# Column sums of every tile at the five block transitions, and the last norm in one pass

## The chip, the cores and the metric

The kernel runs on one core of a Trainium2 chip. The metric is the time of one execution on the device in microseconds (us). The engines are called by their short names: PE is TensorE (matmuls), with PEld for its weight loads, DVE is VectorE, ACT is ScalarE, POOL is GpSimd, and SP issues the DMAs.

## What is computed

Two transformer blocks follow each other on 256 tokens with a model width of 1024, in float32. The first block has two layers, each a mixer (sparse attention in layer 0, differential attention in layer 1) and a squared-ReLU MLP; after each of the four the residual goes through a layer norm. The second block puts 16 meta tokens ahead, and has a mixer and an MLP with RMS norms. The parts that the change touches:

```python
def layer_norm(x, g, b):
    mu = jnp.mean(xf, axis=-1, keepdims=True)
    var = jnp.mean(jnp.square(xf - mu), axis=-1, keepdims=True)
    return ((xf - mu) * lax.rsqrt(var + EPS) * g + b)

# first block, each layer l
        y = ...mixer(modulate(x, sh1, sc1))
        x = layer_norm(ALPHA * x + (1.0 + g1[:, None, :]) * y, ln_g[l, 0], ln_b[l, 0])
        y = sq_relu_mlp(modulate(x, sh2, sc2), mlp_w1[l], mlp_w2[l])
        x = layer_norm(ALPHA * x + (1.0 + g2[:, None, :]) * y, ln_g[l, 1], ln_b[l, 1])

# second block
    h = jnp.concatenate([meta, x], axis=1)
        u = rms_norm_2(h, norm_mix_pre[l])
        proj = u @ w_in[l]
        ...
        h = h + rms_norm_2(mix, norm_mix_post[l])
        u = rms_norm_2(h, norm_mlp_pre[l])
```

Where an RMS norm follows a layer norm (the last layer norm of the first block and the first norm of the second), or where one RMS norm's result is added and goes into the next, the kernel needs the mean square of the second norm's input as well.

## The kernel before

Activations stand feature-major: the residual `xa` is eight tiles of 128 features x 256 tokens. A float32 product is taken as three matmuls on a high and a low half of each operand (`mm3`, lines 387 to 389: high-high, high-low, low-high); the halves of the weights, called `hi` and `lo`, are made on chip from the loaded `raw` by ACT (`cast_hi`) and by DVE or POOL (`cast_lo`, L352).

A *transition* is the end of a projection, the norm behind it, and the start of the next stage. There are five, and all go through `tail`: T0 (attention's output of layer 0), T1 (MLP of layer 0), T2 (differential attention's output of layer 1), T3 (MLP of layer 1, followed by `last_ln`) and T4 (the second block's output projection, followed by `post_norm`). In `tail` PE's order is written by hand: the eight output tiles y are finished in the order m = 0, 2, 4, 6, 1, 3, 5, 7, where n counts them. For n below 4 a tile gets the three matmuls of the last weight; from n = 4 on also those of the weights before it, six or nine in all. Ahead of the last three matmuls of each tile `finish[1](n, m, None)` is called, and after them `finish[1](n, m, y[m])`. DVE, ACT and POOL take their order from a scheduler that walks the program by priorities and dependences.

For the layer norms (`ln_finish`) each finished tile becomes r = y * gate + xa on DVE (`zn`, L633) and its square on ACT (`sq`, L635). The mean and mean square over the 1024 features need sums over partitions and over tiles. `totals` adds the tiles up: r on DVE and sq on POOL (lines 556 and 559, tile `run`). The column sums over partitions are matmuls on PE with the summed tile as weights and a column of ones as the moving operand (`col_sum`, two fp32 matmuls of 128 tokens each, written to a PSUM tile `tr`). They are taken three times for each quantity: for the sum of tiles n = 0 to 3, for that of 4 to 6, and for tile 7. The first stands ahead of the last three matmuls of tile n = 7, the other two behind them, with fillers (`warm`, a matmul of zeros with 512 columns) between. `rstd_rows` makes mean and 1/sigma from the sums and spreads them to rows of all partitions, on PE.

`last_ln` has two passes. It normalizes r in place (L1763, L1766), squares the result times g plus b on ACT (L1768), and takes column sums of all eight squares; from these come the scale of the second norm (`rstd_rows` again), and then the second block's input, `full` (L1779, L1781), with its halves `hh` and `hl`. At the same time POOL makes the new residual `xa` (L1777). The next stage multiplies `hi` and `lo` by `hh` and `hl` (tile `y`), and one feature tile of the weights by the meta tokens repeated eight times, `oh` and `ol` (tile `a`).

The meta tokens' halves `oh` and `ol` are made by POOL in two operations of 128 x 1024, L1704 and L1705, which the program has ahead of the second MLP. `post_norm` sums three quantities: y * post * xa (`full`) on POOL, and y^2 and (y * post)^2 (`sq`, `sqn`) on DVE.

## Time and profile before

| | |
|---|---|
| median of three runs | 1166.39 us (1165.0 to 1170.65) |
| the profiled execution | 1162.97 us |
| its span, first to last instruction | 1161.2 us |
| mean granted clock of PE in it | 0.955 of full speed |
| busy: PE, DVE, ACT, POOL | 92%, 72%, 51%, 23% |
| chain of waits: PE, DVE, DMA, POOL | 68%, 14%, 5%, 5% |

The profile is one execution, whose times are counted from the start of its span. In a timeline a row is one or several equal instructions of an engine, with the start, the time from the first start to the last end, and in brackets how long the engine stood idle before and what it waited for. Matmuls overlap their neighbours, so the price of one is read from the distance of the starts. PEclk in a table of windows is the clock that PE was granted, 1.00 for 2.4 GHz and 0.50 for 1.2 GHz.

### The profile page before, as it was taken

Reading aid. Unit: us, or ns where it says so; the run is one execution under the profiler, and the core shown is the slowest. Engines: PE = TensorE matmul, PEld = TensorE weight load, DVE = VectorE, ACT = ScalarE, POOL = GpSimd, SP = SyncE. Lnnn points to the kernel's source line nnn. Section 1 sums busy time; section 2 is a strip of 40 time slices with the busy share of each in tenths; the row PEclk is TensorE's granted clock in tenths of the full one; section 3 lists DMA queues with packets and bytes.
Section 4 is the critical chain, followed back from the end, with each engine's and each line's share of the span. In section 5 each row is a group of like instructions: output and inputs, shape, how many; then the busy total and the mean of one; then the engine's idle time right before and its main releaser. Section 6 shows DMA issues by size and latency. Waiting matters only on the chain.

```text
span 1161.2 us, 20465 instructions
## 1 busy us (share of the span) xinstructions
PE 1073.1 (92%) x7766; PEld 975.4 (84%) x7766; DVE 840.5 (72%) x1672; ACT 595.3 (51%) x1240; POOL 269.3 (23%) x307
## 2 busy tenths in 40 slices
PE   2789889999999999997999999998899989999996
PEld 1667667999999978896999999887776888899995
DVE  7578985799886677877976555678986677655553
ACT  2456747464445445653754444557365354544442
POOL 3284673100000201324000000336644250000000
PEclk9799888999999989997999999899899997999998
DMA  9977643299996227636587553032120252765621
GB/s 344 316 266 271 210 155 112 89 404 349 331 336 229 97 90 294 211 135 235 202 287 237 183 179 119 1 109 92 55 66 27 92 200 68 252 189 182 189 83 37
DMA packets 60447, 212.58 MB, mean 183 GB/s; under 512 B 6619, under 2 KB 9084, under 8 KB 60348
## 3 DMA queue, kind: packets, MB, share of 16 engines
q1 hardware_dynamic: 59424, 209.43, 51.3%
q0 software_dynamic: 192, 0.79, 0.4%
q8 instruction: 61, 1.00, 0.3%
q10 hardware_dynamic: 732, 1.05, 0.3%
q14 instruction: 38, 0.31, 0.1%
HBM read 209.15 MB, written 1.84 MB: 182 GB/s over the span
## 4 chain that ended last, share of the span: by engine, by line
PE 68%; DVE 14%; DMA 5%; POOL 5%; issue 4%; ACT 3%; POOLq 0%; DVEq 0%; ACTq 0%; SPq 0%
PE y L387 10%; PE y L388 10%; PE y L389 10%; PE pj L387 7%; PE pj L389 7%; PE pj L388 7%; DMA raw<-in_ws 3%; PE tr L392 2%; DVE lo L352 2%; PE y L401 2%; DVE raw L478 1%; PE y L392 1%; PE pj L392 1%; DVE cva L2178 1%; POOL se L1457 1%
## 5 line engine op out<-in xcount | busy, mean ns | idle before, releaser
L366 DVE TENSOR_TENSOR lo<-raw,hi 128x1024 fp32r<-128x1024 f32 (+1 forms) x208 | 226.6, 1105 | 107.0 <-ACT hi L365 106.9
L365 ACT ACTIVATE hi<-raw 128x1024 fp32r<-128x1024 f32 (+1 forms) x208 | 195.3, 959 | 94.1 <-PE pj L388 76.4
L387 PE MATMUL pj<-hh,hi 128*128 128x256 f32 x768 | 216.7, 282 | 0.3
L388 PE MATMUL pj<-hl,hi 128*128 128x256 f32 x768 | 216.6, 282 | 0.2 <-DVE hl L611 0.2
L389 PE MATMUL pj<-hh,lo 128*128 128x256 f32 x768 | 215.7, 281 | 0.0
L352 DVE TENSOR_TENSOR lo<-raw,hi 128x1024 fp32r<-128x1024 f32 (+2 forms) x103 | 126.6, 1236 | 42.2 <-ACT hi L347 40.8
L387 PEld LDWEIGHTS pj<-hh,hi 128*128 128x128 f32 x768 | 145.1, 189 | 2.5 <-ACT relu L807 0.9
L388 PEld LDWEIGHTS pj<-hl,hi 128*128 128x128 f32 x768 | 144.9, 189 | 1.6 <-DVE hl L611 0.4
L389 PEld LDWEIGHTS pj<-hh,lo 128*128 128x128 f32 x768 | 145.2, 189 | 0.0
L388 PE MATMUL y<-actl,hi 128*128 128x256 f32 x512 | 144.3, 282 | 0.8 <-DVE actl L810 0.7
L387 PE MATMUL y<-acth,hi 128*128 128x256 f32 x512 | 144.0, 281 | 0.0
L389 PE MATMUL y<-acth,lo 128*128 128x256 f32 x512 | 143.7, 281 | 0.0
L352 POOL TENSOR_TENSOR lo<-raw,hi 128x512 fp32r<-128x512 f32 (+3 forms) x28 | 47.5, 1703 | 357.9 <-ACT hi L347 335.9
L347 ACT ACTIVATE hi<-raw 128x1024 fp32r<-128x1024 f32 (+2 forms) x107 | 110.8, 1043 | 27.1 <-DMA raw<-in_ws 16.1
L478 DVE CUSTOM_DVE_ANT_0 raw<-raw,cact 128x1024 f32<-128x1024 f32 x75 | 97.1, 1303 | 2.7 <-DMA raw<-in_ws 2.7
L388 PEld LDWEIGHTS y<-actl,hi 128*128 128x128 f32 x512 | 96.9, 189 | 1.5 <-DVE actl L810 1.4
L387 PEld LDWEIGHTS y<-acth,hi 128*128 128x128 f32 x512 | 97.1, 190 | 0.1
L389 PEld LDWEIGHTS y<-acth,lo 128*128 128x128 f32 x512 | 96.8, 189 | 0.0
L388 PE MATMUL y<-hl,hi 128*128 128x256 f32 x296 | 84.5, 286 | 0.0
L387 PE MATMUL y<-hh,hi 128*128 128x256 f32 x264 | 79.7, 302 | 3.9 <-ACT f L1588 2.2
L809 ACT ACTIVATE acth<-act 128x256 fp32r<-128x256 f32 x96 | 39.4, 416 | 83.5 <-DVE act L808 83.5
L389 PE MATMUL y<-hh,lo 128*128 128x256 f32 x264 | 76.8, 291 | 0.0
(658 smaller groups left out, 2486.3 us busy)
## 6 DMA issues: line engine op xcount, KB each, us to landing
raw<-in_ws SPq DMA_DIRECT2D x372, 512.0 KB, 4.7
bm<-bscr SPq DMA_DIRECT2D x4, 512.0 KB, 14.6
raw<-in_ws SPq DMA_DIRECT2D x4, 416.0 KB, 8.7
bm<-in_ws SPq DMA_DIRECT2D x3, 512.0 KB, 8.2
raw<-in_ws SPq DMA_DIRECT2D x3, 408.0 KB, 3.7
zn<-in_ws SPq DMA_DIRECT2D x2, 512.0 KB, 6.6
xa<-in_xT SPq DMA_DIRECT2D x2, 512.0 KB, 6.6
oh<-in_ws SPq DMA_DIRECT2D x2, 512.0 KB, 7.3
```

What stands on the lines that cost most here:

```text
L347: return self.nc.scalar.activation(w[1], w[0], AF.Copy)
L352: return eng.tensor_tensor(w[2][:, a:b], w[0][:, a:b], w[1][:, a:b].bitcast(F32), op=OP.subtract)
L365: i = nc.scalar.activation(hi[:, a:b], raw[:, a:b], AF.Copy)
L366: j = (lo_by or nc.vector).tensor_tensor(lo[:, a:b], raw[:, a:b], hi[:, a:b].bitcast(F32), op=OP.subtract)
L387: mm(out, lh, rh, start=start, stop=False, skip_group_check=True)
L388: mm(out, lh, rl, start=False, stop=False, skip_group_check=True)
L389: mm(out, ll, rh, start=False, stop=stop, skip_group_check=True)
L392: self.nc.tensor.matmul(out, l, r, start=start, stop=stop, skip_group_check=True)
L401: last = self.nc.tensor.matmul(out, l, r, start=start, stop=stop, skip_group_check=True)
L478: nc.vector.tensor_tensor_reduce(out=raw, in0=raw, in1=self.cact, op0=OP.mult, op1=OP.add, scale=0.5, scalar=0.0, accum_out=t)
L809: nc.scalar.activation(ah, f, AF.Copy)
L1457: nc.gpsimd.tensor_scalar(es[g][:, sl], es[g][:, sl], sm[:, tb, g:g + 1], 1.0, op0=OP.mult, op1=OP.mult)
```

## The change

`totals` no longer adds tiles up. Every finished tile gets its own column sums on PE, two tiles later: ahead of the last three matmuls of tile n those of tile n - 2 are issued, and behind tile 7 those of tiles 6 and 7, with one filler between where there were two ahead. The running adds of DVE and POOL are gone in all five transitions.

In `tail` the `lo` half of the second following weight is made by DVE and not by POOL. `oh` and `ol` are made in 16 operations of 128 x 128 by a generator, `meta_eight`, which the program calls piece by piece in the second MLP (POOL's place for them is the scheduler's, below); to that end `mlp` takes `more`, and the ticks that feed the pieces come closer together.

`last_ln` has one pass. It takes weighted column sums in the same pass as the plain ones: the moving operand is no longer a column of ones but three columns (1, g^2, g*b) for r and two (1, g^2) for its square. The mean square of the second norm's input is computed from these sums in small column operations, with constants that `meta_prep` prepares in 13 more DVE operations. Both scales and the mean are spread to rows before the tiles are touched, and normalizing, `xa`, `full` and its halves are done in one loop.

```diff
@@ -545,25 +545,19 @@
-    def totals(self, s, i, eng):
-
...
+    def totals(self, s, *cols):
+
+
+        todo = []
+
+        def add(n, *xs):
+            todo.append((n, xs))
+
+        def rest(until):
+            while todo and todo[0][0] <= until:
+                n, xs = todo.pop(0)
+                for i, x in zip(cols, xs):
+                    self.col_sum(s, i, x, n == 7)
 
         return add, rest
 
@@ -621,26 +615,21 @@
             c.gate = self.need(*gate)
             c.mod = mod()
             c.s = self.col_stats(1e-5)
-            c.one, c.two = self.totals(c.s, 0, nc.vector), self.totals(c.s, 2, nc.gpsimd)
+            c.add, c.rest = self.totals(c.s, 0, 2)
 
         def tile_(n, m, y):
             if y is None:
-                if n == 7:
-                    c.one[1]()
-                    c.two[1]()
+                c.rest(n - 2)
                 return
             r = c.r
             nc.vector.scalar_tensor_tensor(r[m], y, c.gate[:, m:m + 1], self.xa[:, m, :], op0=OP.mult, op1=OP.add)
             sq = self.T(self.lnp, (128, 256), "sq", bufs=3)
             nc.scalar.activation(sq, r[m], AF.Square)
-            c.one[0](n, r[m])
-            c.two[0](n, sq)
+            c.add(n, r[m], sq)
             if n == 7:
-                c.one[1]()
-                c.two[1]()
-                self.warm(2)
-                c.one[1]()
-                c.two[1]()
+                c.rest(6)
+                self.warm(1)
+                c.rest(7)
 
         def end(work):
             next(work, None)
@@ -708,9 +697,9 @@
-            for w, e in zip(nx, (nc.vector, nc.gpsimd)):
+            for w in nx[:2]:
                 self.cast_hi(w)
-                self.cast_lo(w, e)
+                self.cast_lo(w, nc.vector)
@@ -830,12 +819,12 @@
-    def mlp(self, l, finish, following, vectors):
+    def mlp(self, l, finish, following, vectors, more=()):
 
         pend = self.mlp_head(l)
         y = self.y_tiles()
-        self.fill = self.chain(*(self.ada(*lv) for lv in vectors), self.fill)
-        n = 8 * len(vectors) + 8
+        self.fill = self.chain(*(self.ada(*lv) for lv in vectors), self.fill, more)
+        n = 8 * len(vectors) + (24 if more else 8)
         for j in range(4, 31):
             self.tick(n * (j - 3) // 26 - n * (j - 4) // 26)
             late = True if j > 28 else None
@@ -1696,16 +1685,22 @@
-            self.mrep = [self.T(self.acts, (128, 8, 128), tag, F32R) for tag in ("oh", "ol")]
-            mh, ml = (t.rearrange("p k (e t) -> p k e t", e=8) for t in self.mrep)
-            meta = self.metaT[:, :, None, :].to_broadcast([128, 8, 8, 16])
-            with self.fenced():
-                nc.gpsimd.tensor_copy(mh, meta)
-                nc.gpsimd.tensor_tensor(ml, meta, mh.bitcast(F32), op=OP.subtract)
             self.mlp(1, self.last_ln((1, 5)), ['b_t0', 'b_t1', 'b_t2', 'b_c4', 'b_q0', 'b_c5', 'b_q1', 'b_c6'],
-                     ((1, 5),))
+                     ((1, 5),), more=self.meta_eight())
         return True
+
+    def meta_eight(self):
+
+        nc = self.nc
+        self.mrep = [self.T(self.acts, (128, 8, 128), tag, F32R) for tag in ("oh", "ol")]
+        mh, ml = (t.rearrange("p k (e t) -> p k e t", e=8) for t in self.mrep)
+        meta = self.metaT[:, :, None, :].to_broadcast([128, 8, 8, 16])
+        for k in range(8):
+            with self.after(1):
+                nc.gpsimd.tensor_copy(mh[:, k], meta[:, k])
+            yield
+            nc.gpsimd.tensor_tensor(ml[:, k], meta[:, k], mh[:, k].bitcast(F32), op=OP.subtract)
+            yield
 
 
...
@@ -1753,40 +1764,86 @@
 
     def last_ln(self, gate):
 
+
         nc = self.nc
         g, b = self.lncol[:, 6, :], self.lncol[:, 7, :]
-
...
+        c = SimpleNamespace(todo=[])
+
+        def begin():
+            z = [self.T(self.resid, (128, 4, 256), "zn", bufs=2) for _ in range(2)]
+            c.r = [z[m // 4][:, m % 4, :] for m in range(8)]
+            c.gate = self.need(*gate)
+            c.s = self.PS("tr")
+            self.mm(c.s[:, 0:13], self.ones, self.lnw0, True, False)
+
+        def rest(until):
+            while c.todo and c.todo[0][0] <= until:
+                n, m, sq = c.todo.pop(0)
+                for tb in range(2):
+                    ts, o = slice(128 * tb, 128 * tb + 128), 5 * tb
+                    self.mm(c.s[:, o:o + 3], c.r[m][:, ts], self.lnw[:, m, 0:3], False, n == 7)
+                    self.mm(c.s[:, o + 3:o + 5], sq[:, ts], self.lnw[:, m, 0:2], False, n == 7)
+
+        def tile_(n, m, y):
+            if y is None:
+                rest(n - 2)
+                return
+            nc.vector.scalar_tensor_tensor(c.r[m], y, c.gate[:, m:m + 1], self.xa[:, m, :], op0=OP.mult, op1=OP.add)
+            sq = self.T(self.lnp, (128, 256), "sq", bufs=3)
+            nc.scalar.activation(sq, c.r[m], AF.Square)
+            c.todo.append((n, m, sq))
+            if n == 7:
+                rest(6)
+                self.warm(1)
+                rest(7)
+
+        def end(work):
+            r, s = c.r, c.s[:, 0:10].rearrange("p (t j) -> p j t", t=2)
+            c2 = lambda tag: self.T(self.small, (128, 2), tag, bufs=2)
+            mu, m2, va, rs, t, q, rr = (c2(x) for x in ("lmu", "m2", "va", "rso", "lt", "lq", "rro"))
+            xx = self.xx = self.T(self.small, (128, 2), "xx", bufs=1)
+            k = self.T(self.small, (128, 3), "lnk", bufs=1)
+            nc.vector.tensor_scalar(mu, s[:, 0], 1.0 / 1024, None, op0=OP.mult)
+            nc.vector.tensor_mul(m2, mu, mu)
+            nc.vector.scalar_tensor_tensor(va, s[:, 3], 1.0 / 1024, m2, op0=OP.mult, op1=OP.subtract)
+            nc.gpsimd.tensor_tensor(rs, va, self.mhalf[:, 0:2], op=OP.pow)
+            mur = self.rows_of(mu, "y0")
+
+            nc.vector.tensor_copy(k, c.s[:, 10:13])
+            nc.vector.tensor_mul(t, mu, s[:, 1])
+            nc.vector.scalar_tensor_tensor(m2, m2, k[:, 0:1], s[:, 4], op0=OP.mult, op1=OP.add)
+            nc.vector.scalar_tensor_tensor(t, t, -2.0, m2, op0=OP.mult, op1=OP.add)
+            nc.vector.scalar_tensor_tensor(q, mu, k[:, 1:2], s[:, 2], op0=OP.mult, op1=OP.add)
+            rsr = self.rows_of(rs, "y1")
+            nc.vector.tensor_mul(t, t, rs)
+            nc.vector.scalar_tensor_tensor(t, q, 2.0, t, op0=OP.mult, op1=OP.add)
+            nc.vector.tensor_mul(t, t, rs)
+            nc.vector.tensor_scalar(xx, t, k[:, 2:3], None, op0=OP.add)
+            nc.vector.tensor_scalar(va, xx, 1.0 / 1024, None, op0=OP.mult)
+            nc.gpsimd.tensor_tensor(rr, va, self.mhalf[:, 0:2], op=OP.pow)
+            self.warm(4)
+            rrr = self.rows_of(rr)
+            self.warm(3)
+            full = {}
+            for m in range(11):
                 if m < 8:
...
+                    nc.vector.tensor_sub(r[m], r[m], mur)
+                if 1 <= m < 9:
+                    n = m - 1
+                    nc.vector.tensor_mul(r[n], r[n], rsr)
+                    nc.gpsimd.tensor_scalar(self.xa[:, n, :], r[n], g[:, n:n + 1], b[:, n:n + 1], op0=OP.mult, op1=OP.add)
+                    full[n] = self.T(self.lnp, (128, 256), "full", bufs=3)
+                    nc.scalar.activation(full[n], r[n], AF.Identity, scale=self.gbw[:, 0, n:n + 1],
+                                         bias=self.gbw[:, 1, n:n + 1])
+                if 2 <= m < 10:
+                    nc.vector.tensor_mul(full[m - 2], full[m - 2], rrr)
+                if m > 2:
+                    self.normed_halves(m - 3, full[m - 3], 16)
+                if m in (1, 2, 5):
                     next(work, None)
             self.split(self.hh[:, :, 0:16], self.hl[:, :, 0:16], self.metaT)
 
-        return self.ln_finish(gate, lambda: apply)
+        return begin, tile_, end
@@ -1853,16 +1910,11 @@
         def begin():
             c.s = self.PS("tr")
             self.mm(c.s[:, 0:6], self.ones, self.epsw, True, False)
-            c.sums = [self.totals(c.s, 2 * i, nc.vector if i else nc.gpsimd) for i in range(3)]
-
-        def rest():
-            for x in c.sums:
-                x[1]()
+            c.add, c.rest = self.totals(c.s, 0, 2, 4)
 
         def tile_(n, m, y):
             if y is None:
-                if n == 7:
-                    rest()
+                c.rest(n - 2)
                 return
             ys[m] = y
 
@@ -1870,12 +1922,11 @@
             nc.vector.scalar_tensor_tensor(xs[0], y, post[:, m:m + 1], self.xa[:, m, :], op0=OP.mult, op1=OP.mult)
             nc.scalar.activation(xs[1], y, AF.Square)
             nc.scalar.activation(xs[2], y, AF.Square, scale=post[:, m:m + 1])
-            for x, t in zip(c.sums, xs):
-                x[0](n, t)
+            c.add(n, *xs)
...
```

Left out of the diff are the lines of `meta_prep` that fill `lnw` (1, g^2 and g*b for each feature) and `lnw0` (their sums and the epsilons), and the end of `post_norm`, which issues `c.rest(6)`, a filler and `c.rest(7)` as `ln_finish` does.

On PE, T2, the last two tiles of y before: `oh`, `ol` are the activations here and `hi`, `lo` the weights, `tr` the PSUM tile of the sums, `run` the sums of several tiles.

```order
L387 MATMUL y_1193_6017<-oh_4858,hi_1215_6182 128x256
L388 MATMUL y_1193_6017<-ol_4859,hi_1215_6182 128x256
L389 MATMUL y_1193_6017<-oh_4858,lo_1216_6183 128x256
L392 MATMUL tr_6176<-ones_85,run_1239_6250 128x1 x2
L392 MATMUL tr_6176<-ones_85,run_1240_6252 128x1 x2
L387 MATMUL y_1193_6017<-oh_4858,hi_1218_6190 128x256
L388 MATMUL y_1193_6017<-ol_4859,hi_1218_6190 128x256
L389 MATMUL y_1193_6017<-oh_4858,lo_1219_6191 128x256
L392 MATMUL tr_6176<-ones_85,run_1245_6289 128x1 x2
L392 MATMUL tr_6176<-ones_85,run_1246_6291 128x1 x2
```

The same place after: `zn` is r of one tile, `sq` its square.

```order
L392 MATMUL tr_6201<-ones_85,zn_6194 128x1 x2
L392 MATMUL tr_6201<-ones_85,sq_6310 128x1 x2
L387 MATMUL y_1187_6041<-oh_4868,hi_1213_6215 128x256
L388 MATMUL y_1187_6041<-ol_4869,hi_1213_6215 128x256
L389 MATMUL y_1187_6041<-oh_4868,lo_1214_6216 128x256
L387 MATMUL y_1188_6042<-oh_4868,hi_1210_6207 128x256
L388 MATMUL y_1188_6042<-ol_4869,hi_1210_6207 128x256
L389 MATMUL y_1188_6042<-oh_4868,lo_1211_6208 128x256
L392 MATMUL tr_6201<-ones_85,zn_6194 128x1 x2
L392 MATMUL tr_6201<-ones_85,sq_6320 128x1 x2
L387 MATMUL y_1188_6042<-oh_4868,hi_1213_6215 128x256
L388 MATMUL y_1188_6042<-ol_4869,hi_1213_6215 128x256
```

Where two column sums stood before the last matmuls of the last tile alone, two now stand ahead of the last matmuls of each tile.

On POOL, T2, before: the second weight's `lo`, the running sums of the squares, and the two operations on the meta tokens between them.

```order
L352 TENSOR_TENSOR lo_1225_6203<-raw_1223_6200,hi_1224_6202 128x1024
L556 TENSOR_TENSOR run_1240_6252<-sq_6242,sq_6248 128x256
L559 TENSOR_TENSOR run_1240_6252<-run_1240_6252,sq_6261 128x256
L559 TENSOR_TENSOR run_1240_6252<-run_1240_6252,sq_6272 128x256
L1704 CAST oh_6395<-metaT_4864 128x1024
L556 TENSOR_TENSOR run_1246_6291<-sq_6281,sq_6287 128x256
L1705 TENSOR_TENSOR ol_6396<-metaT_4864,oh_6395 128x1024
L559 TENSOR_TENSOR run_1246_6291<-run_1246_6291,sq_6300 128x256
```

On POOL after, from the attention of layer 1 (`dr`) to the scale of T2's norm (`st`, a power of the variance `va`).

```order
L1665 TENSOR_TENSOR dr_1196_6099<-dss_6077,mhalf_83 128x4
L1700 CAST oh_7599<-metaT_4874 128x128 x2
L1702 TENSOR_TENSOR ol_7600<-metaT_4874,oh_7599 128x128 x2
L1700 CAST oh_7599<-metaT_4874 128x128 x2
L1702 TENSOR_TENSOR ol_7600<-metaT_4874,oh_7599 128x128 x2
L1700 CAST oh_7599<-metaT_4874 128x128 x2
L1702 TENSOR_TENSOR ol_7600<-metaT_4874,oh_7599 128x128 x2
L1700 CAST oh_7599<-metaT_4874 128x128 x2
L1702 TENSOR_TENSOR ol_7600<-metaT_4874,oh_7599 128x128 x2
L585 TENSOR_TENSOR st_6359<-va_6360,mhalf_83 128x2
```

The sums are gone; the meta tokens' pieces, sixteen operations in all, now stand ahead of the power. The first of them waits for the last matmul of y, as the buffer of `oh` held the activations before.

On DVE, T3, the end of the normalizing and the start of the second norm's products before: `y` is the mean or the scale in rows, `full` the product's input, the last `tr` the row of the second scale.

```order
L1766 TENSOR_TENSOR zn_8510<-zn_8510,y_1649_8739 128x256 x2
L1772 COPY xx_8799<-tr_8748 128x2
L590 TENSOR_SCALAR va_8802<-tr_8748 128x2
L1781 TENSOR_TENSOR full_8814<-full_8814,tr_8805 128x256
L1781 TENSOR_TENSOR full_8818<-full_8818,tr_8805 128x256
L1781 TENSOR_TENSOR full_8824<-full_8824,tr_8805 128x256
L1751 TENSOR_TENSOR hl_119<-full_8814,hh_118 128x256
L1751 TENSOR_TENSOR hl_119<-full_8818,hh_118 128x256
L1751 TENSOR_TENSOR hl_119<-full_8824,hh_118 128x256
L1781 TENSOR_TENSOR full_8830<-full_8830,tr_8805 128x256
```

The last twelve of the same loop after: `tr_8811` is the row of the second scale.

```order
L1839 TENSOR_TENSOR full_8850<-full_8850,tr_8811 128x256
L1762 TENSOR_TENSOR hl_119<-full_8842,hh_118 128x256
L1830 TENSOR_TENSOR zn_8554<-zn_8554,y_1641_8790 128x256
L1833 TENSOR_TENSOR zn_8554<-zn_8554,y_1642_8798 128x256
L1839 TENSOR_TENSOR full_8859<-full_8859,tr_8811 128x256
L1762 TENSOR_TENSOR hl_119<-full_8850,hh_118 128x256
L1833 TENSOR_TENSOR zn_8554<-zn_8554,y_1642_8798 128x256
L1839 TENSOR_TENSOR full_8867<-full_8867,tr_8811 128x256
L1762 TENSOR_TENSOR hl_119<-full_8859,hh_118 128x256
L1839 TENSOR_TENSOR full_8874<-full_8874,tr_8811 128x256
L1762 TENSOR_TENSOR hl_119<-full_8867,hh_118 128x256
L1762 TENSOR_TENSOR hl_119<-full_8874,hh_118 128x256
```

Normalizing (L1830, L1833), product (L1839) and low half (L1762) now alternate tile by tile, so that the last product comes third from the end. On PE the stage's first six matmuls go to `y`, and the seventh to `a`, whose PSUM bank `tr_8811` held before.

## Rows read from the trace of the kernel before

**Rows 1.** The page: busy time of each engine, share of the span, instructions.
```profile
PE 1073.1 (92%) x7766; PEld 975.4 (84%) x7766; DVE 840.5 (72%) x1672; ACT 595.3 (51%) x1240; POOL 269.3 (23%) x307
```

**Rows 2.** Windows: length, busy time by engine, granted clock, DMA share, GB/s.
```profile
core 0: us, PE busy (x) PEld busy (x) DVE busy (x) ACT busy (x) POOL busy (x), PEclk, DMA share, GB/s
208.00:214.50 6.50, 6.50 (x61) 6.50 (x59) 5.85 (x13) 2.81 (x7) 3.67 (x5) 1.00 0.00 0
399.00:405.20 6.20, 6.20 (x55) 6.20 (x54) 5.55 (x12) 2.84 (x7) 3.07 (x5) 1.00 0.02 4
...
538.00:550.50 12.50, 8.41 (x31) 6.38 (x32) 7.02 (x12) 1.01 (x3) 5.75 (x5) 0.50 0.26 99
...
600.00:700.00 100.00, 100.00 (x846) 100.00 (x846) 59.52 (x80) 47.56 (x71) 0.00 (x0) 1.00 0.61 204
...
745.00:751.90 6.90, 5.80 (x23) 4.46 (x23) 3.43 (x11) 2.95 (x9) 0.70 (x1) 0.51 0.01 4
...
948.50:953.00 4.50, 2.36 (x16) 1.75 (x15) 4.50 (x8) 3.19 (x7) 2.03 (x3) 1.00 1.01 393
...
956.70:964.00 7.30, 7.30 (x34) 6.59 (x33) 2.79 (x7) 1.28 (x4) 0.61 (x2) 0.50 0.26 93
```

**Rows 3.** Timeline of PE, T1: start, us, instruction, count, [idle before <-releaser].
```profile
404.01 0.95 PE L392 MATMUL tr<-ones,run 128*128 128x1 f32 x8
404.82 0.36 PE L387 MATMUL y<-acth,hi 128*128 128x256 f32 x1
405.02 0.28 PE L388 MATMUL y<-actl,hi 128*128 128x256 f32 x1
405.14 0.28 PE L389 MATMUL y<-acth,lo 128*128 128x256 f32 x1
```

**Rows 4.** Timeline of PE, T2: the four idle times.
```profile
532.00 0.38 PE L387 MATMUL y<-oh,hi 128*128 128x256 f32 x1 [0.74 <-DVE zn L633]
...
534.66 0.39 PE L387 MATMUL y<-oh,hi 128*128 128x256 f32 x1 [1.57 <-DVE zn L633]
...
538.65 1.01 PE L392 MATMUL tr<-ones,run 128*128 128x1 f32 x4 [1.44 <-DVE run L559]
543.10 1.01 PE L392 MATMUL tr<-ones,run 128*128 128x1 f32 x4 [3.44 <-POOL run L559]
```

**Rows 5.** Timeline of POOL and of ACT, T2.
```profile
537.28 1.04 POOL L1704 CAST oh<-metaT 128x1024 fp32r<-128x1024 f32 x1 [1.29 <-PE y L389]
538.28 0.90 POOL L556 TENSOR_TENSOR run<-sq,sq 128x256 f32<-128x256 f32 x1
539.14 2.77 POOL L1705 TENSOR_TENSOR ol<-metaT,oh 128x1024 fp32r<-128x1024 f32 x1
...
539.21 0.42 ACT L635 ACTIVATE sq<-zn 128x256 f32<-128x256 f32 x1 [2.58 <-POOL run L556]
```

**Rows 6.** Timeline of PE, T4.
```profile
951.00 0.39 PE L387 MATMUL y<-oh,hi 128*128 128x256 f32 x1 [2.00 <-ACT sqn L1872]
...
954.86 0.39 PE L387 MATMUL y<-oh,hi 128*128 128x256 f32 x1 [1.14 <-ACT sqn L1872]
...
957.94 2.55 PE L392 MATMUL tr<-ones,run 128*128 128x1 f32 x12
960.35 1.01 PE L392 MATMUL pj<-zero 128*128 128x512 bf16 x2
```

**Rows 7.** Timeline of PE, T3: the stage behind last_ln begins.
```profile
750.02 0.79 PE L387 MATMUL y<-hi,hh 128*128 128x272 f32 x1
...
751.51 0.43 PE L389 MATMUL y<-hi,hl 128*128 128x272 f32 x1
751.74 0.37 PE L387 MATMUL a<-hi,oh 128*128 128x272 f32 x1
```

**Rows 8.** Timeline of DVE, T3: the first norm's statistics, the second norm's products.
```profile
736.50 0.16 DVE L585 TENSOR_SCALAR st<-tr 128x2 f32<-128x2 f32 x1 [1.62 <-PE tr L392]
...
748.55 1.08 DVE L1781 TENSOR_TENSOR full<-full,tr 128x256 f32<-128x256 f32 x3 [2.16 <-PE tr L392]
749.55 1.09 DVE L1751 TENSOR_TENSOR hl<-full,hh 128x256 fp32r<-128x256 f32 x3
```

62 lines of the change are left out of this document (18 added, 44 removed).

## Prediction

> **What bounds the kernel now.** I read the page first, then the timeline and the waits around the five places that the change touches, then the granted clock there. [rows 1] shows TensorE (PE) busy for 92% of the span, VectorE (DVE) for 72%, GpSimd (POOL) for 23%. An average does not price this change, since only the five transitions are touched. I number them T0 (near 208 us), T1 (399), T2 (529), T3 (728) and T4 (949): T0 to T2 are the attention and MLP ends that go through a layer norm, T3 is the second MLP's end, which last_ln serves, and T4 is the second block's output projection, which post_norm serves.
>
> They are of two kinds. In T0, T1 and T3 TensorE has no idle time at all while the eight tiles of y are finished: in [rows 2] it is busy for 6.50 of 6.50 us, and 6.20 of 6.20 us, at granted clock 1.00. VectorE is close behind (5.85, 5.55). There any instruction added to TensorE's queue ahead of the last tile moves the end by its own length. In T2 and T4 TensorE waits: [rows 4] has idle times of 0.74, 1.57, 1.44 and 3.44 us, the last of them for a running sum on POOL, and [rows 6] 2.00 and 1.14 us behind the second square. Right after the transitions the granted clock is at its lower level, 1.2 GHz: 0.50 over 538 to 550.5 us and over 956.7 to 964 us, 0.51 over 745 to 751.9 us [rows 2].
>
> **The price of a sum.** A column sum of one quantity of one tile is two fp32 matmuls with the tile as weights, which the trace shows as four passes. Before a transition's last tile eight of them stand in a row: they begin at 404.01, the next matmul of y begins at 404.82, and the one after it 0.20 later where 0.12 is usual [rows 3]. So a group of eight costs 0.81 + 0.08 = 0.89 us at 2.4 GHz, 0.10 us a pass. At 1.2 GHz twelve passes take from 957.94 to 960.35 [rows 6], 0.20 us a pass, so a group of eight costs about 1.7 us and one of twelve 2.41 us. A wide matmul follows the one before it by 0.12 us at the higher level (256 columns, 405.02 to 405.14, [rows 3]) and by 0.23 at the lower (272 columns, 751.51 to 751.74, [rows 7]), so each one issued at the lower level costs 0.1 us more.
>
> At this point a page speaks for the change. The row shows 0.10 us a pass [rows 3]. The Trainium skill ("TensorE: Matmul & The Clock Gate", section "Back-to-back issue gap") gives a matmul of 1 to 64 columns a floor of about 25 ns, and the section "LDWEIGHTS (loading the stationary operand)" gives about 107 ns for 128 weight columns, as an estimate from its P/1.2. The row agrees with the second: it is the weights that are paid for here, not the one column. By the first alone the added sums would cost a quarter, and the result would be the third rival below.
>
> **The change, part by part.** Before, a quantity is summed over tiles by running adds on VectorE or POOL, and TensorE takes three column sums of it; after, eight. With two quantities that is 10 more column sums, 40 passes, five groups of eight for each of T0 to T3; with three quantities in T4 it is 60 passes, five groups of twelve.
>
> *T0 and T1.* Five groups by 0.89 are 4.45 us on the path, since TensorE is dense there. The first group also waits for the first square, which the running adds did not: about 0.4 us, the length of a square on ScalarE [rows 5]. One filler matmul of two is dropped, -0.2. Each: **+4.65**. The adds that VectorE and POOL lose give nothing back here: TensorE has no idle time for them to end. The second weight's cast_lo comes to VectorE, but takes the place of the adds.
>
> *T2.* The four waits of [rows 4] add up to 7.19 us. Their largest cause is that two POOL copies of the meta tokens, 1.04 and 2.77 us, stand between POOL's running adds [rows 5]. Without the adds nobody waits for them there. They do not leave, though: in POOL's new order their sixteen pieces stand behind the last matmul of y (whose operand's buffer they take over) and ahead of the power that makes the scale of this very norm. So the power waits for them. An eighth of the two copies each, 8 x (0.13 + 0.35), would be 3.8 us; an add of twice the width takes 0.90 [rows 5], which with 0.5 for a copy bounds them above at 11. I take 5.4: the eighths and 0.1 us of fixed cost for each of sixteen operations (an estimate). The power is wanted 2.75 us after the last tile at the higher clock level, 5.0 us at the lower (16 passes, a filler, three short VectorE operations). So the copies cost about 2.6 us at the higher level and 0.4 at the lower.
>
> If the clock stayed high: 4.45 + 0.4 - 7.19, some 2 us less because the final sums now run at the lower level and would not, and the 2.6: -1.75. If it falls early, at about 533.5: two groups at 0.89, three at 1.7, the group ahead of the last tile +0.8, some 18 wide matmuls by 0.1 and the 0.4 make 9.9, less 7.19, plus 0.4 for the copies: +3.1. I take **+3**, because from 531 to 534 TensorE would do little but wait for squares and load weights for single columns, and stretches of that kind are where the rows lose the clock: 538 to 550.5 us is mostly idle or narrow and stands at 0.50 [rows 2]. With the copies at 11 us it would be +8.5.
>
> *T3, first part.* Like T0: +4.65.
>
> *T3, last_ln.* Its second pass over the eight tiles goes. Now the statistics are ready at 736.50, the product with the second norm's scale begins at 748.55 [rows 8] and the next stage's first matmul at 750.02 [rows 7]. Without the pass there remain 16 short VectorE operations (0.16 us each, as in [rows 8]), POOL's second power behind two of its eight tile operations, and the row broadcast. By my count the product starts 5.0 us earlier and the first matmul 5.3 us earlier, at 744.7. But after six matmuls the stage takes `a`, 751.74 in [rows 7], whose PSUM bank is the one that now holds the broadcast row of the second norm, and which is free only after the last of the eight products. In VectorE's new order that product is the 22nd operation from there; three of them take 1.00 us (748.55 to 749.55, [rows 8]), so it ends near 743.5 + 22 x 0.335 = 750.9, and `a` starts near 751.0 where it started at 751.74. Of 5.3 us, 0.7 is left; and while TensorE waits, the clock is likely to stay low for a while, 0.5. T3 in all: 4.65 - 0.7 + 0.5 = **+4.5**, between +4 and +5.5, and -0.6 if `a` does not bind.
>
> *T4.* At the higher level: five groups of twelve (60 x 0.10 + five gaps of 0.08) are 6.5, the first wait for the second square 0.55, and some 1.8 of the 3.14 us of waits in [rows 6] are filled; the final sums, now at 0.50, would take 2.7 us less: +2.5. At the lower level from about 954: two groups at 1.3, three at 2.5, the next one +1.0, some 30 wide matmuls by 0.1, less 1.8, plus 0.55: about +12.5, with nothing gained behind. TensorE is busy only 2.36 of 4.50 us between 948.5 and 953 [rows 2] and gets more narrow passes right behind that, where before wide matmuls followed. I take **+12**.
>
> *The rest.* meta_prep gains 13 VectorE operations on small tiles at about 0.2 us each: between 0 (they run beside attention work) and +2.6; I take **+0.5**. The change of the ada loads' order lies inside the MLP's dense stretch, 0 unless TensorE has to wait there.
>
> **Sum.** 4.65 + 4.65 + 3 + 4.5 + 12 + 0.5 = 29.3 us on the profiled execution's 1162.97 us: 1192.3. The median of the three runs is 1166.39, 3.4 us above that execution, so a median may come out as much higher; I say **1192**.
>
> **Rivals.**
> 1. The clock holds through T2 and T4. For it: before, it held at 1.00 over 948.5 to 953 us though TensorE was half idle [rows 2]. Then 4.65 + 4.65 - 1.75 + 4.0 + 2.5 + 0.5 = 14.55: **1177.5**; with the copies at their lower bound, 1176.
> 2. The clock falls in T0, T1 and T3 as well, since the wide matmuls there are thinned by narrow passes. Three groups in each at 1.7 and not 0.89 (2.4) and some 22 wide matmuls by 0.1 (2.2) are 4.6 each, 13.8 together: **1206**. Against it: TensorE stays without idle time there.
> 3. Faster than before: the narrow passes are nearly free, because their weight loads run under the matmuls ahead of them, as the weight loads of wide matmuls do now. All five places together add 220 passes, 22.3 us at 0.1015. With the clock high, the total of +14.55 turns negative once two thirds of that hide; with three quarters hidden it is 14.55 - 16.7 = -2.2, 1160.8, with all of it -7.75, **1155**. Against it: [rows 3] measures the price behind wide matmuls in this very place, and eight passes stand in a row after the change too, so at most the first of each group hides. (The Trainium skill's 25 ns for a narrow matmul, in the section on the issue gap named above, would come to the same as three quarters hidden.)
> 4. The wait of `a` does not bind (VectorE runs ahead, or the next operation there is released otherwise): T3 keeps 5 us, 29.3 - 5 = 24.3: **1187**.
>
> **How the numbers follow.** Half a per cent, 5.8 us, is about what a measurement of this kernel can tell from no change. Forecast 0.52 (own range 1186 to 1198), rival 1 0.17, rival 2 0.13, rival 3 0.08, rival 4 0.10. The range reaches from a little below rival 1 to rival 2, 1173 to 1207. Faster by more than 5.8 us is most of rival 3, 0.07; within it the rest of rival 3 and the low end of rival 1, 0.10; slower 0.83.
>
> **What would show it.** T0 and T1: y's last tile 4.5 to 5 us later after the first product, TensorE without idle time, eight-pass groups at 0.81. T2: no wait for POOL ahead of the last tile, the clock at 0.5 before it, and the power starting when the sixteen copies end. T3: `a` waits for VectorE's last product, 6 matmuls after the stage's start. T4: the statistics 10 us or more later, granted clock 0.5 from before the fifth tile. I am wrong if T4's groups of twelve run at 1.2 us (rival 1), or if a group of eight is followed by y in clearly less than 0.8 us (rival 3).

## The result, and the profile after

The changed kernel takes 1201.8 us (median of four runs, 1200.39 to 1203.72) where the kernel before takes 1168.18 in four runs on the same chip (1165.0 to 1170.65): a ratio of 1.0283, 95% interval 1.0254 to 1.0312. So it is slower, as forecast, and 9.8 us above the predicted 1192: inside the range of 1173 to 1207, but above the 1186 to 1198 that the forecast gave its own mechanism. Half of the 9.8 us is the base: 29.3 us were added to one execution of 1162.97, and the median of before is now 5.2 above that execution. The other half, 4.3 us, is in the terms: the medians lie 33.6 apart. The two profiled executions (1162.97 and 1203.03) lie 40.1 apart, and part of that is chance, as a second profile of before shows below.

The page of after: busy time, share of the span (1201.2 us, mean granted clock 0.940 where it was 0.955) and instructions.

```profile
PE 1109.7 (92%) x7944; PEld 1014.8 (84%) x7944; DVE 826.4 (69%) x1667; ACT 592.9 (49%) x1232; POOL 238.6 (20%) x291
```

TensorE has 36.6 us more work than in [rows 1] in 178 more instructions (220 passes are added, the 32 of the second pass over the tiles and some fillers are gone), and is as dense. At 0.10 us each the 178 would be 18 us; the rest I put down to matmuls at the lower clock, which I did not add up. VectorE and POOL have less work, and no gain from it shows. The windows at T1, T2, T3 and T4 show the clock (length, busy time by engine, granted clock, DMA share, GB/s):

```profile
409.00:419.40 10.40, 10.40 (x92) 10.40 (x91) 3.19 (x7) 2.89 (x7) 0.00 (x0) 1.00 0.00 0
...
541.00:546.20 5.20, 2.92 (x27) 2.83 (x26) 3.45 (x5) 3.79 (x5) 0.00 (x0) 1.00 1.02 396
546.20:562.60 16.40, 16.40 (x80) 16.22 (x78) 3.79 (x8) 2.50 (x6) 3.41 (x11) 0.50 0.53 210
...
764.60:772.70 8.10, 2.90 (x10) 1.60 (x7) 7.88 (x23) 5.34 (x13) 3.71 (x5) 0.50 0.00 1
772.70:778.30 5.60, 5.55 (x24) 5.58 (x25) 0.66 (x2) 0.77 (x2) 1.89 (x14) 0.50 0.01 3
...
976.30:979.70 3.40, 2.06 (x16) 1.98 (x17) 2.18 (x5) 2.33 (x5) 0.00 (x0) 1.00 1.02 395
979.70:1004.70 25.00, 25.00 (x120) 24.86 (x118) 2.90 (x6) 4.50 (x12) 0.00 (x0) 0.50 0.22 91
```

T1 is dense at 1.00, as [rows 2] has it before, only longer. T2 and T4 begin at 1.00 with TensorE half idle, then are dense at 0.50 to the end. At T3 TensorE is busy for 2.90 of the 8.10 us of the first window, and the matmuls that follow are still at 0.50.

The groups of sums: TensorE in T1, then in T4 (start, length, instruction, count).

```profile
409.77 0.50 PE L392 MATMUL tr<-ones,zn 128*128 128x1 f32 x4
410.13 0.58 PE L392 MATMUL tr<-ones,sq 128*128 128x1 f32 x4
410.57 0.36 PE L387 MATMUL y<-acth,hi 128*128 128x256 f32 x1
410.77 0.28 PE L388 MATMUL y<-actl,hi 128*128 128x256 f32 x1
...
980.79 0.84 PE L392 MATMUL tr<-ones,full 128*128 128x1 f32 x4
981.50 0.99 PE L392 MATMUL tr<-ones,sq 128*128 128x1 f32 x4
982.36 0.99 PE L392 MATMUL tr<-ones,sqn 128*128 128x1 f32 x4
983.21 0.56 PE L387 MATMUL y<-oh,hi 128*128 128x256 f32 x1
```

A group of eight takes 0.80 us (409.77 to 410.57), and of the two matmuls behind it the second follows the first by 0.20: the two numbers of [rows 3] are 0.81 and 0.20. A group of twelve takes 2.42 us (980.79 to 983.21), the 2.41 of [rows 6].

For what follows I cut each execution at the same instructions. "T0" to "T4" is the time from VectorE's first product of a finished tile to the transition's statistics; "second block's mixer" is the time from T3's statistics to T4's first product. In us:

| kernel | T0 | T1 | T2 | T3 | T4 | second block's mixer |
|---|---|---|---|---|---|---|
| before | 8.37 | 9.15 | 17.60 | 8.39 | 14.06 | 213.21 |
| before, second profile | 8.58 | 9.67 | 18.34 | 8.38 | 15.63 | 214.15 |
| after | 12.67 | 12.53 | 18.81 | 12.63 | 28.43 | 217.31 |

### The profile page after: what moved, and what is told of

Read it like the earlier page. It is cut to its first block, busy times and chain, and to the rows that moved or that the text cites. A ratio compares the mean times of both kernels' runs of the same rounds, so it can differ in the third digit from the quotient of the medians.

```text
span 1201.2 us, 20764 instructions
## 1 busy us (share of the span) xinstructions
PE 1109.7 (92%) x7944; PEld 1014.8 (84%) x7944; DVE 826.4 (69%) x1667; ACT 592.9 (49%) x1232; POOL 238.6 (20%) x291
## 3 DMA queue, kind: packets, MB, share of 16 engines
HBM read 209.15 MB, written 1.84 MB: 176 GB/s over the span
## 4 chain that ended last, share of the span: by engine, by line
PE 48%; issue 17%; DVE 9%; POOL 3%; ACT 2%; DMA 2%; POOLq 0%; SPq 0%; DVEq 0%; ACTq 0%
PE y L387 7%; PE y L388 7%; PE y L389 7%; PE pj L387 5%; PE pj L388 5%; PE pj L389 5%; PE tr L392 3%; PE y L401 1%; DVE lo L352 1%; DVE cva L2229 1%; PE y L392 1%; DMA raw<-in_ws 1%; PE d L392 1%; PE sc L392 1%; POOL se L1627 1%
## 5 line engine op out<-in xcount | busy, mean ns | idle before, releaser
L796 ACT ACTIVATE relu<-pj 128x256 f32<-128x256 f32 x96 | 35.1, 372 | 60.1 <-PE pj L389 60.1
```

Source lines behind the costliest of these rows:

```text
L796: nc.scalar.activation(r, p, AF.Relu)
```

## Experiments: T4

**The kernel before, once more** (e0). It has no edit. It is there for the spread of a profile.

> The kernel before, once more, for a second profile of it. Theory (how often the clock falls in the second block's mixer, between T3 and T4, is chance: it differs between executions of one kernel): from the stage's first matmul behind T3 to T4's first product this execution takes 199.7 us or 2 to 4 us more, with other low stretches than the 6.8 us at 833.8. Rival (the change makes the mixer slower by itself): 199.7 us within 0.5, with the same low stretches.

Measured: 1166.81 us. The stretches differ from the first profile by 0.0 to 1.6 us each. So I read nothing into a difference below 2 us that only two profiles show. (For T4 the spread is larger: b2, below, has the T4 of before and takes 12.58 us there.) The expectation of a longer mixer was wrong in this profile; it came in a later one with the same mixer code (b2, below).

**T4's sums as before, the rest as after** (e1).

```diff
-            c.add, c.rest = self.totals(c.s, 0, 2, 4)
+            c.add, c.rest = self.totals_old(c.s, (0, nc.gpsimd), (2, nc.vector), (4, nc.vector))
...
-                self.warm(1)
+                self.warm(2)
                 c.rest(7)
```

Here `totals_old` holds the running adds and the three column sums of before.

> The changed kernel with the sums of T4 alone as before: running adds on VectorE and POOL, three column sums of each quantity. Theory (T4 costs 12 to 15 us, mostly because its narrow passes run at the lower clock level from 980 us on): 14.4 us come back, 1187 us (1185 to 1190), and the granted clock of T4 stays at 1.00 until after the last tile. Rival (T4's loss is only the 60 passes at 0.10 us, less the waits they fill, and the clock would have fallen anyway): 2.5 us come back, 1199.

Measured: 1189.96 us (1185.06 to 1201.72), 1.0214 of before [1.0143, 1.0285], 11.8 below after, though the two intervals overlap; T4 takes 15.64 us. Its windows in T4:

```profile
973.90:977.10 3.20, 1.74 (x10) 1.33 (x11) 3.20 (x8) 2.65 (x7) 1.84 (x2) 0.99 1.02 399
977.10:989.50 12.40, 11.85 (x56) 11.13 (x54) 6.45 (x15) 3.52 (x10) 2.37 (x3) 0.50 0.46 179
```

The clock fell here too, at 977.1, with the sums of before: my expectation of 1.00 was wrong. It still takes no longer than the second profile of before. So the lower clock is not made by the added passes alone; what they do is multiply its price. Sixty passes at 0.20 us (2.42 by twelve, above) are 12.1 us, and T4 differs by 28.43 - 15.64 = 12.8.

**Fillers in T4** (e3). In `post_norm`, matmuls of zeros with 512 columns between the groups of sums.

```diff
             if y is None:
+                if n == 2:
+                    self.warm(12)
                 c.rest(n - 2)
+                if n > 1:
+                    self.warm(2)
                 return
```

> The changed kernel with more work on TensorE in T4: 12 fillers of 512 columns ahead of the first column sums, where it stands idle for 3.1 us, and two behind each group of sums, 24 in all. Theory (the clock is the cause: T4 would cost little if TensorE had dense work in it): the granted clock stays at 1.00 through T4 or falls later, the statistics come 6 to 9 us earlier although 24 fillers by 0.21 us are added, 1193 to 1196 us. Rival (the number of passes is the cause): the fillers only add, 2 us or more, 1204 to 1210 us, with the clock at 0.50 as before.

Measured: 1198.2 us (1192.66 to 1204.39), 1.026 [1.0209, 1.0312]; T4 takes 19.13 us.

```profile
977.20:993.50 16.30, 16.23 (x136) 14.91 (x134) 4.95 (x11) 5.99 (x17) 0.00 (x0) 1.00 0.53 215
993.50:1000.30 6.80, 6.22 (x26) 4.92 (x25) 2.29 (x10) 0.62 (x2) 1.40 (x2) 0.50 0.00 0
```

The same sums with more matmuls between them take 9.3 us less, because the clock stays at 1.00 until 993.5. The six profiles that have these sums in T4 without fillers take 26.7 to 28.4 us there, so this is no chance of one profile: the low clock is shown as the cause of 9.3 us of T4's length. The median is above the 1193 to 1196 expected. The medians differ by 3.6 us only, and their intervals overlap, so a gain of the whole kernel is not shown; the profile's span is 8.5 shorter.

## Experiments: T0 to T2

**Sums of T0 to T2 as before** (e6). The edit in `ln_finish` is that of T4's experiment, with two quantities:

```diff
-            c.add, c.rest = self.totals(c.s, 0, 2)
+            c.add, c.rest = self.totals_old(c.s, (0, nc.vector), (2, nc.gpsimd))
```

> The changed kernel with the sums of T0, T1 and T2 as before: running adds on VectorE and POOL, three column sums of each quantity; T3, T4 and the rest as changed. Theory: T0 gives back 4.3, T1 3.4, T2 some 4, in all 11 to 13 us, 1189 to 1191 us. Rival (POOL's adds bring T2's waits back, now with the copies of the meta tokens): T2 gives nothing back, 1194 us.

Measured: 1185.08 us (1182.35 to 1187.14), 1.0145 [1.0114, 1.0176], 16.7 below after. T0 8.99, T1 8.39, T2 13.94: 12.7 us less than after in these three stretches, as expected; the median fell by more than that, and the rest is spread over the stages between, where one execution can't tell it from chance. The rival (T2 gives nothing back) is out: 13.94 us is also less than the 17.60 of before.

**The second `lo` on POOL again** (e4).

```diff
-            for w in nx[:2]:
+            for w, e in zip(nx, (nc.vector, nc.gpsimd)):
                 self.cast_hi(w)
-                self.cast_lo(w, nc.vector)
+                self.cast_lo(w, e)
```

> The changed kernel with the low half of the second following weight on POOL again, as before. Theory: it matters at T2 alone, where its loads come late; the first product there starts 1 to 2 us earlier than in the changed kernel, measured from the end of T1, and T0, T1, T3 and T4 take the same; 1 to 2 us in all, hardly to be told from 1201.8 by the times. Rival (VectorE needs the 1.2 us everywhere): each transition 1 us shorter, 1197.

Measured: 1202.72 us (1194.72 to 1206.9), 1.029 [1.0237, 1.0343]: no gain. Two things cancel in its profile. From T1's next stage to T2's first product it takes 108.75 us, where after takes 112.18. But T1 takes 18.13 and T2 20.54:

```profile
408.00:413.80 5.80, 5.80 (x53) 5.80 (x52) 2.10 (x5) 1.64 (x4) 0.00 (x0) 1.00 0.00 0
413.80:426.00 12.20, 12.20 (x59) 12.04 (x58) 1.57 (x4) 1.67 (x4) 0.00 (x0) 0.50 0.00 0
```

This is rival 2 in T1: TensorE is busy for 5.80 of 5.80 us, and then the clock falls.

**The pieces of `oh` and `ol` behind T2's power** (e5).

```diff
-        nc.gpsimd.tensor_tensor(st[:, 2:4], va, self.mhalf[:, 0:2], op=OP.pow)
+        self.scale_op = nc.gpsimd.tensor_tensor(st[:, 2:4], va, self.mhalf[:, 0:2], op=OP.pow)
...
-            with self.after(1):
+            with self.tc.issue_after(self.scale_op.ins):
                 nc.gpsimd.tensor_copy(mh[:, k], meta[:, k])
```

> The changed kernel with one difference in POOL's order: the sixteen pieces of the meta tokens' copies stand behind T2's power instead of ahead of it. Theory: the power, which waits 0.57 us for the pieces now, starts right behind the variance, and T2 is 0.5 to 1.2 us shorter from the statistics to the next matmul. Rival (the pieces cost nothing where they are): no difference there.

Measured: 1197.83 us in one run. Its POOL in T2, and its TensorE windows in T1:

```profile
559.80 0.70 POOL L585 TENSOR_TENSOR st<-va,mhalf 128x2 f32<-128x2 f32 x1 [28.97 <-DVE va L581]
560.46 0.54 POOL L1700 CAST oh<-metaT 128x128 fp32r<-128x128 f32 x2
...
402.40:408.30 5.90, 5.90 (x54) 5.90 (x53) 2.17 (x5) 1.64 (x4) 0.00 (x0) 1.00 0.00 0
408.30:420.60 12.30, 12.30 (x59) 12.11 (x58) 1.61 (x5) 1.67 (x4) 0.00 (x0) 0.50 0.00 0
```

The power waits for its variance and for nothing else. From the statistics to the next stage T2 takes 4.17 us, where after takes 5.33: the pieces cost about 1.2 in after. The other profiles bear it out: 5.33 to 5.60 in all seven with the pieces ahead of the power, 4.17 to 4.19 in all five with the pieces or the copies behind it. T1 fell again (18.16), with code that is the same there as in after.

## Experiments: T3

**Another bank for the row of the second scale** (e2).

```diff
-            rrr = self.rows_of(rr)
+            rrr = self.rows_of(rr, "pj")
```

> The changed kernel with one difference: the row of the second norm's scale in T3 stands in another PSUM bank (one of the two of pj), so that the stage's matmuls into a need not wait for VectorE's last product. Theory (that wait, 5.24 us, eats the gain of the single pass): the stage goes on after its first six matmuls, paced by VectorE's tiles (1.67 us for each), 4 to 6 us come back, 1196 to 1198 us. Rival (VectorE's loop sets the end of the stage whatever a waits for): 0 to 1.5 us, 1200 to 1202.

Measured: 1197.27 us (1193.27 to 1202.25), 1.0253 [1.0214, 1.0292]. The interval overlaps that of after, so the 4.5 us between the medians are not shown as a gain. First TensorE in T3 of after, then of this kernel:

```profile
765.68 0.59 PE L387 MATMUL y<-hi,hh 128*128 128x272 f32 x1
...
767.08 0.43 PE L389 MATMUL y<-hi,hl 128*128 128x272 f32 x1
772.75 0.56 PE L387 MATMUL a<-hi,oh 128*128 128x272 f32 x1 [5.24 <-DVE full L1839]
```

```profile
761.24 0.59 PE L387 MATMUL y<-hi,hh 128*128 128x272 f32 x1 [0.30 <-ACT hh L1761]
...
762.63 0.43 PE L389 MATMUL y<-hi,hl 128*128 128x272 f32 x1
762.86 0.43 PE L387 MATMUL a<-hi,oh 128*128 128x272 f32 x1
```

The wait of 5.24 us is gone with the bank, so the bank was its cause. The last matmul into `a`, near the end of the stage, starts 17.00 us after the statistics, where it started 23.47 after them in before and 24.47 in after. By T4's first product little of it is left (216.30 us in the mixer's column, against 217.31 in after). Behind the last `a` this profile stands at 0.50 in four stretches (781 to 788, 815 to 822, 849 to 856 and 870 to 884), 34.1 us in all, and after in three, 17.1 us in all; what that costs stands under T3 in the account of the prediction.

**Two passes in `last_ln`, with the new sums** (e7). `last_ln` is the function of before, and ends in `ln_finish`.

```diff
+        def apply(r, mu, rs, work):
+            s = self.col_stats(1e-6)
...
-        return begin, tile_, end
+        return self.ln_finish(gate, lambda: apply)
```

> The changed kernel with last_ln as before, in two passes (its first pass with the sums of every tile, as the other layer norms of the changed kernel have them). Theory (the single pass gains 6.9 us at the stage's first matmul and loses it again to the wait of a for VectorE's last product and to the lower clock behind it): from T3's statistics to T4's first product the time is 213 to 217 us against 217.3 with the single pass; the whole is the same within what can be told, 1198 to 1203 us. Rival (the single pass is a gain of its own, some 5 us): 1205 to 1208.

Measured: 1200.91 us (1197.31 to 1208.66), 1.029 [1.0256, 1.0323]; mixer's column 217.11, where after has 217.31. So the single pass, as it was built, gains nothing that can be measured.

## Experiments: what is worth keeping

**The copies of before, behind T2's power,** in the kernel before (b2):

```diff
-            with self.fenced():
+            with tc.issue_after(self.scale_op.ins):
                 nc.gpsimd.tensor_copy(mh, meta)
```

> The kernel before with one difference in POOL's order: the two copies of the meta tokens (1.04 and 2.77 us) stand behind T2's power instead of between its running adds. Theory (they hold up the adds, and these the last column sums): the waits of 1.44 and 3.44 us in T2 shrink to under 1 us together, T2 takes 3.5 to 5 us less, 0.3 to 0.4% faster than before. Rival (what is late next is almost as late, or the copies then collide with VectorE's work behind the power): 0 to 1.5 us.

Measured: 1163.89 us (1158.17 to 1171.11), 0.9982 [0.9955, 1.0009]; T2 takes 14.46 us. TensorE and POOL in T2:

```profile
540.48 1.87 PE L392 MATMUL tr<-ones,run 128*128 128x1 f32 x8 [0.91 <-DVE run L559]
...
545.38 0.71 POOL L591 TENSOR_TENSOR st<-va,mhalf 128x2 f32<-128x2 f32 x1 [6.07 <-DVE va L587]
546.05 1.04 POOL L1704 CAST oh<-metaT 128x1024 fp32r<-128x1024 f32 x1
```

Of the waits for running sums in [rows 4], 1.44 and 3.44 us, one of 0.91 is left, and T2 is 3.1 to 3.9 us shorter. The whole kernel's interval still reaches 1, so the 0.3 to 0.4% expected is not shown: in this profile the mixer's column has 217.10, with before's code there.

**The best parts** (b1): running adds as before in T0, T1, T2 and T4, and the second `lo` on POOL as before; from the change the single pass with its weighted sums, with the row in the other bank and the pieces behind T2's power. These two edits (the others stand above):

```diff
-            rrr = self.rows_of(rr)
+            rrr = self.rows_of(rr, "pj")
...
-            with self.after(1):
+            with self.tc.issue_after(self.scale_op.ins):
```

> The single pass of last_ln with its row in a bank of pj, and the copies of the meta tokens behind T2's power; the sums of T0, T1, T2 and T4 and the second weight's low half as before. Theory: T2 takes 3 to 4 us less than before, T3's sums cost 4.2, the stage behind it begins 6.8 earlier and is not held up; 4 to 6 us less than before, 1161 to 1163 us. Rival (the second block's mixer takes back what T3 gains, as its clock falls more often when it starts earlier): 1164 to 1168 us, no better than moving the copies alone.

Measured: 1163.04 us (1158.25 to 1165.92, ten runs), 0.9954 [0.9939, 0.9970]. TensorE behind `last_ln`:

```profile
744.01 0.39 PE L387 MATMUL y<-hi,hh 128*128 128x272 f32 x1 [0.38 <-ACT hh L1799]
...
745.17 0.28 PE L387 MATMUL a<-hi,oh 128*128 128x272 f32 x1
```

`a` follows 1.16 us behind the first matmul with no wait. The mixer's column is 210.62, below every other profile shown so far. T0 to T4: 8.44, 8.89, 13.65, 12.62, 15.64.

**Fillers with the running sums** (b3, b4). The kernel of b2 with matmuls of zeros in T2 (behind tiles 5 and 6) and T4 (behind 3 and 6), then the same two lines in the kernel of b1:

```diff
+            if gate == (1, 2):
+                self.warm({5: 4, 6: 6}.get(n, 0))
...
+            self.warm({3: 9, 6: 4}.get(n, 0))
```

> The kernel before with the copies of the meta tokens behind T2's power, and with 23 fillers of 512 columns where TensorE waits: in T2 four behind tile n = 5 and six behind n = 6, in T4 nine behind n = 3 and four behind n = 6. Theory (the idle time in T2 and T4 brings the clock down, and the rest of the transition pays for it): the granted clock stays at 1.00 through T2 or T4, each of them 2 to 4 us shorter than without fillers; 1158 to 1161 us. Rival (the clock falls in the final sums anyway, and fillers that outlast a wait delay the next matmul): 1164 to 1167.

> The kernel of b1_best_parts (single pass of last_ln with its row in a bank of pj, the copies of the meta tokens behind T2's power, the other sums as before) with the 23 fillers of b3_fill. Theory (the two gains stand in different places and add up): T2 5 us shorter than before and T4 0 to 2, T3 as in b1_best_parts; 1159 to 1161 us. Rival (what is gained ahead of the second block's mixer is lost in it, where the clock falls by chance): 1162 to 1164, the same as either alone.

Measured: on b2 1163.02 us, 0.9961 [0.9941, 0.9981], T2 12.39, T4 13.66; on b1 1160.66 us (1156.55 to 1168.01, twelve runs), 0.9953 [0.9927, 0.9978], T2 13.11, T4 14.44. T2 and T4 of the second:

```profile
529.40:540.50 11.10, 9.17 (x62) 6.81 (x61) 9.70 (x17) 5.18 (x11) 8.00 (x6) 1.00 1.01 404
...
947.80:956.90 9.10, 7.45 (x49) 5.33 (x47) 8.73 (x19) 4.90 (x14) 4.50 (x5) 1.00 0.93 366
```

The last kernel is about half a per cent faster than the kernel before, and the clock stands at 1.00 in these two windows. It is not clearly faster than b1 without fillers, and b3 is not clearly faster than b2. Of b3's expected gains T2's is there (14.46 us in b2, 12.39 in b3), T4's is not (12.58 in b2, 13.66 in b3). So in T4 fillers on top of the running sums are not shown to gain anything.

## Why the prediction came out as it did

**The whole.** The parts account for it: with the sums of T4 taken back the median falls by 11.8 us (e1), with those of T0 to T2 by 16.7 (e6), and T3's cost 4.24 in its profile, together 32.7 of the 33.6 us. The forecast's sum came near in part because misses of either sign meet: T0 and T1 came out some 2 us below their terms, T2, T3 and T4 above.

**What bounds it.** Right. T1 is still dense, 10.40 of 10.40 us, and every added pass moves the end.

**The price of a sum.** Right: 0.80 and 2.42 us for the groups, where 0.81 and 2.41 were foreseen. Rival 3 (free passes) is out by these rows.

**T0 and T1, +4.65 each.** T0 +4.1 to +4.3, T1 +2.9 to +3.4 against the two profiles of before. The mechanism is right; T0's term was 0.4 to 0.6 us too large and T1's 1.3 to 1.8. In T1 the difference lies mostly in before, whose clock fell 1.1 us ahead of T1's statistics:

```profile
407.20:408.30 1.10, 1.10 (x7) 1.02 (x6) 0.00 (x0) 0.00 (x0) 0.00 (x0) 0.50 0.00 0
```

The forecast had T1 of before at 1.00. In e6, which has the sums of before in T1 and stays at 1.00 there, T1 takes 8.39 us, and after takes 4.1 more, as in T0. (One line ahead of the prediction has to be corrected: the matmuls of the earlier weights go to the tiles with m of 4 or more, which are n = 2, 3, 6 and 7, not to all from n = 4 on. No term rested on it.)

**"The second weight's cast_lo comes to VectorE, but takes the place of the adds".** This step failed in T2. ScalarE, VectorE, TensorE and POOL there, in after:

```profile
541.57 1.06 ACT L347 ACTIVATE hi<-raw 128x1024 fp32r<-128x1024 f32 x1 [2.01 <-DMA raw<-in_ws]
...
542.66 1.23 DVE L352 TENSOR_TENSOR lo<-raw,hi 128x1024 fp32r<-128x1024 f32 x1 [1.84 <-ACT hi L347]
543.80 0.87 DVE L625 SCALAR_TENSOR_TENSOR zn<-y,mod,xa 128x256 f32<-128x256 f32 x2
...
544.34 0.61 PE L392 MATMUL tr<-ones,zn 128*128 128x1 f32 x4 [2.28 <-DVE zn L625]
...
559.19 0.54 POOL L1700 CAST oh<-metaT 128x128 fp32r<-128x128 f32 x2 [26.70 <-PE y L389]
...
562.80 0.82 DVE L580 TENSOR_TENSOR m<-st 128x2 f32<-128x2 f32 x1
...
563.57 0.86 POOL L1702 TENSOR_TENSOR ol<-metaT,oh 128x128 fp32r<-128x128 f32 x2
563.65 0.16 DVE L581 SCALAR_TENSOR_TENSOR va<-tr,m 128x2 f32<-128x2 f32 x1
...
564.38 0.70 POOL L585 TENSOR_TENSOR st<-va,mhalf 128x2 f32<-128x2 f32 x1
```

The `lo` stands ahead of the first product on VectorE, not where the adds were, and itself waits 1.84 us for ACT, whose `hi` had waited 2.01 for the weight's load. So the first product is late, and TensorE stands idle for 2.28 us until it is there. From T1's next stage (its first matmul into `y`) to that product the seven profiles with the `lo` on VectorE take 110.6 to 112.2 us (mean 111.4), the seven with it on POOL 108.8 to 111.3 (mean 109.9). That is some 1.5 us, with ranges that overlap.

**T2, +3.** From its first product to the next stage +2.4, with the late `lo` +4.65 (109.97 us to the first product before, 112.18 after); by the second profile of before the whole is +3.25. The clock fell as foreseen, only earlier: at 546.2, 2.4 us behind the first product where 4.6 was assumed. The pieces take 5.24 us (559.19 to 564.43), where 5.4 was estimated, and the power stands 0.57 behind its variance (ready at 563.81), where 0.4 was. They cost more than that wait, though: the second of VectorE's three short operations takes 0.82 us beside them, where it takes 0.16 in e5, and together this is the 1.2 us that e5 gets back.

**T3, +4.5.** Its sums cost +4.24, as foreseen. The wait of `a` did bind, as the forecast had it: rival 4 is out. `a` starts 1.5 us earlier against the statistics than before (0.7 was foreseen). The term that failed is the 0.5 for the clock: it stays at 0.50 until 778.3, behind 24 matmuls more, which costs about 2.4. What comes behind, in the mixer, was put at nothing, and after has three stretches there at half clock, one of them:

```profile
856.80:863.60 6.80, 6.55 (x29) 6.55 (x30) 6.18 (x17) 2.08 (x4) 5.19 (x9) 0.50 0.26 80
```

By the mixer's column the kernels with the new sums in T3 take 216.3 to 218.4 us (eight profiles, b1 and b4 aside), those with before's `last_ln` and sums 213.2 to 217.1 (four). So T3 and what follows came to 3 to 4 us above my term. To see where, cut the column at the last matmul into `a`. From there to T4's first product, in before, after, b1 and e2:

```profile
759.97:949.69 189.72, 172.68 (x1273) 152.27 (x1271) 152.55 (x360) 102.22 (x267) 91.51 (x98) 0.98 0.24 82
...
783.49:976.32 192.83, 175.88 (x1261) 155.09 (x1259) 153.98 (x362) 101.24 (x266) 88.91 (x97) 0.96 0.25 80
...
753.50:947.53 194.03, 177.42 (x1273) 156.64 (x1271) 153.46 (x360) 102.38 (x268) 91.61 (x100) 0.96 0.25 81
...
771.56:970.86 199.30, 183.15 (x1261) 161.65 (x1259) 153.29 (x361) 102.30 (x267) 89.31 (x97) 0.91 0.23 79
```

This part's length goes with the time that the clock is at 0.50 in it: 189.7 to 190.0 us in the three profiles with 6.8 us at 0.50, 192.8 to 194.0 in the ten with 17.1 us, 199.3 in e2 with 34.1 us. One of the ten is b2 (193.5), with the `last_ln` and the mixer of before. So some 3 us of after's excess are the clock in the mixer. Three of the four profiles with before's T3 have the 6.8 us and none of the other ten, but whether the change makes the clock fall there, or chance did, is not shown.

Ahead of that cut the kernels differ by their code: from T3's statistics to the last `a` it is 23.5 to 24.2 us with before's T3, 24.05 with the two passes of e7, 24.3 to 25.0 in the six with the single pass and the wait of `a`, and 16.6 to 17.0 in the three with the other bank (e2, b1, b4). So the single pass does gain some 7 us where `a` need not wait; b1 keeps 6.5 of it to T4's first product against b2, with the same 17.1 us at 0.50 behind it, and e2 lost it to the clock.

**T4, +12.** +12.8 to +14.4 against the two profiles of before. (The forecast's terms for the lower level add up to 12.85, where it has 12.5; of the higher level's, five groups are 6.4 and not 6.5.) The mechanism (low clock, twice the price of each pass) is shown by the sums of before (15.64) and by the fillers (19.13). The clock fell 3.4 us behind the first product and not 4.3, so that all groups but the first ran at half, which the term had for three of five; that is why it was too small.

**The rest, +0.5.** The operations of `meta_prep` on the new constants stand at 477.2 to 478.0 us in after, between T1 and T2, and no cost of theirs shows: e4, which has them, takes 108.8 us there, before 110.0. MLP0, between T0 and T1, was in no term, and takes 3.7 us more in after. It holds a stretch at half clock which is dense:

```profile
245.80:249.20 3.40, 3.40 (x18) 3.40 (x17) 3.40 (x8) 2.68 (x7) 0.00 (x0) 0.50 1.02 412
```

Two other kernels of the seven with the new sums in T0 and T1 have it too; four have the stage only 0.5 to 1.2 us longer. I count it as chance.

**Rival 2** (the clock falls in the dense transitions too) did not happen in the profile of after, and did in T1 of three other profiles with the same sums: 18.13, 18.16 and 17.21 us where four have 12.53. That is +4.7 to +5.6, near the 4.6 worked out for one transition. In T0 it happened in none of the seven (12.62 to 12.67 us). So for T1 the forecast and rival 2 are not two outcomes of the kernel, but of an execution. Its chance of 0.13 was for all three places at once; for T1 alone three in seven is what the profiles have. Rival 1 is out as well: the groups of twelve in T4 take 2.42 us and not 1.2.
